# Hybrid decoder step: where one piece of query weights is staged, and when three groups of small instructions are issued

## The chip, the core and the metric

The kernel runs on one core of a Trainium2 chip. The metric is the device time of one execution in microseconds (us), the median of several runs. The core has a matrix engine (PE), a vector engine (DVE), a scalar engine (ACT), a general engine (POOL) and a queue engine (SP) that issues most of the DMA transfers. Each engine runs its own list of instructions in order and waits on semaphores for the others.

## The reference, cut to what matters

One layer of a hybrid decoder is computed for a prompt of 1,024 tokens and for 8 single new tokens ("samples") that have 2,048 cached tokens each. The model is 1,024 wide.

- The input is normalised (RMS norm) and multiplied with one matrix `w_in` of 1024 x 3864. Its columns give the gates of a short convolution, the queries (512 columns, eight heads of 64), keys and values of three branches, branch gates and an output gate.
- Queries and keys are normalised per head and rotated by position.
- Each query attends in three branches, which are mixed by sigmoid gates: over compressed blocks (32 tokens are turned into one key and value by the weights `cmp_w`), over the sixteen 64-token blocks that score best, and over a window of 512 tokens.
- The convolution group and the attention group are multiplied by their SiLU gates, put side by side, multiplied by `w_out` and added to the input.
- The samples do the same with cached rows, which are gathered by a page table, and the new cache rows are outputs too.

## The kernel before

Every product is made to nearly full fp32 precision from fast matmuls: each operand is split into a high and a low part (ACT copies the high part with `copy`, line 78, and DVE or POOL subtracts to get the low part with `sub`, line 82), and two or three matmuls are summed in PSUM. Transposes are matmuls against the identity.

**Order.** The Python text is written as several generators that are interleaved (`merge`). The written order is not the final one: when the program is built, a scheduler goes through it with modelled times and fixes each engine's list. An engine gets, among the instructions that the model calls ready, the one written earliest; buffers that share a name are handed out in the order written. So the place of a line sets its priority, and the model's idea of when data land decides the rest. On the chip the lists are then run strictly in order, whatever the real times are.

**Stage 1 (to about 232 us), `phase0` and `chan_stream`.** For each block of input columns the weights come in four pieces (`w_loader`, lines 162 to 191): `fetch` loads a piece of two k-tiles by a DMA of SP (line 171), `split` makes high and low tiles `wh` and `wl` of it. Raw pieces live in two buffers `wraw` and one `wx`; there are nine `wh` and nine `wl`, and a set needs eight. The columns are three key/value branches (`kv_tile`) and two halves of the queries (`q_tile`, the loop `for which in range(2)`), each over nine token tiles; the order of the tiles in the query loop is 0, 1, 2, 3, 8, 4, 5, 6, 7. Between them PE runs chunks of the channel products (`chan_mm`, lines 225 to 227). The weights of the second query half are fetched and split while the first half runs (lines 779 to 788): pieces 0 and 1 into `wraw`, piece 2 into `wx`, and piece 3 into a `wraw` again, after piece 0 is split. In the same loop `w_fetch` and `w_split` split one half of `w_out` and store it in DRAM: k-slices 0, 2, 4, 6 use the two buffers named `rows`, slices 1, 3, 5, 7 the two named `kd2`; a slice takes one buffer for the load and one for its high part.

In the first branch, pairs of token tiles are sent from SBUF to SBUF by four DMAs (`token_pairs`, line 432) and then transposed on PE (`cmp_transposes`, line 440). That second step is queued in a list `posts` with a count; every call of `posted(1)` takes one off, and what reaches zero is written out there (line 657). `small_things`, in the step of tile 7, queues `indices` with a count of 1: six small matmuls (lines 507 and 510). Both take PSUM banks of the name `tp`.

**Stage 2 (to about 660 us)** is the prompt's attention, with the convolution beside it.

**Stage 3 (about 670 to 790 us), `cmp_stream`**, builds the samples' compressed keys: in 16 steps, step n starts the gather of rows n + 2 into one of two buffers `raw`, `regroup(n + 1)` copies the next rows into one of two buffers `reg` (half by ACT, line 78, half by POOL, line 79, two copies each), and then four groups of four transposes (line 1149) and their products with `cmp_w` (line 1170) follow. Output products of the prompt (`out_tile`, lines 1582 to 1584) fill PE between them.

**Stage 4 (to the end), `sample_stream`**: for every 512 cached keys and each half h of the samples `keys` makes scores, `weigh` the softmax, and `values` transposes the weights into `ptz` (ACT line 78 for the high part, DVE line 82 for the low part) and multiplies them with the values (line 1466, 16 matmuls). After the last `values` an end part (lines 1498 to 1515) scales and sums the branches for h = 0 and for h = 1 on DVE and ACT and transposes the result on PE; the samples' output product (line 1617) follows. The prompt's last output tiles fill PE here too.

Of the kernel before, what the change touches and what calls it, by code (L numbers as in the profile page):

```python
# [10 lines left out]
F32 = mybir.dt.float32  # L11
# [50 lines left out]
def hymba_step_kernel(ctx, tc, io):  # L62
    nc = tc.nc
    WARM = 8

# [97 lines left out]
    def w_loader(wp, n, kp, raw_bufs, hk, hl_bufs, lo_eng=POOL):  # L163


        def load(col, width):
            hs, ls, raws = [], [], []

            def fetch(i, home=wp, name="wraw"):
                r = home.tile([128, kp, n], F32, name=name, bufs=raw_bufs if name == "wraw" else 1)  # L170
                SP.dma_start(r[:, :, :width], w_in[:, i * kp:(i + 1) * kp, col:col + width])
                raws.append(r)

            def split(i, eh=ACT, el=lo_eng):
                for j in range(0, kp, hk):
                    r = raws[i][:, j:j + hk, :width]
                    h = wp.tile([128, hk, n], F32R, name="wh", bufs=hl_bufs)
                    l = wp.tile([128, hk, n], F32R, name="wl", bufs=hl_bufs)
                    copy(eh, h[:, :, :width], r)
                    sub(el[j // hk % len(el)] if isinstance(el, tuple) else el, l[:, :, :width], r, f(h[:, :, :width]))  # L180
                    hs.append(h)
                    ls.append(l)

            def tiles(k):
                return hs[k // hk][:, k % hk, :width], ls[k // hk][:, k % hk, :width]

            return tiles, fetch, split
# [167 lines left out]
    ROWS, ENDS = 2, 14000  # L355
# [253 lines left out]
    def phase0():  # L609
# [36 lines left out]
        for t in range(NT):  # L646
# [9 lines left out]
            if rows is not None and t < 8:  # L656
                posts.append((lambda pr=token_pairs(rows, t - 1), t=t: cmp_transposes(pr, t - 1), 4 if t < 5 else 3 if t < 7 else 1))
# [110 lines left out]
        for which in range(2):  # L768
            w = nxt[0]
            nxt = wl0(COL_Q + 256, 256)  # L770
            for t in (0, 1, 2, 3, 8, 4, 5, 6, 7):
# [7 lines left out]
                if which == 0:  # L779
                    if t == 0:  # L780
                        for i in range(2):
                            nxt[1](i)
                        nxt[1](2, wk, "wx")
                    if t == 2:
                        nxt[2](0, ACT, EL)
                        nxt[1](3)
                    if t in (3, 4, 5):
                        nxt[2](t - 2, ACT, EL)
# [342 lines left out]
    def cmp_stream():  # L1131
# [64 lines left out]
        for n in range(16):  # L1196
            if n + 2 < 16:
                gather(n + 2)
            if n + 1 < 16:
                regroup(n + 1)  # L1200
# [6 lines left out]
            for j in range(2):  # L1207
                for rp in range(2):
# [92 lines left out]
    def sample_stream():  # L1301
# [135 lines left out]

        def values(c, h, Sb):
# [10 lines left out]
            sub(DVE, pz[:, :, 4:32:9, :], pv, f(pz[:, :, 0:28:9, :]))  # L1449
# [51 lines left out]
        for h in range(2):  # L1501
# [13 lines left out]
            PE.transpose(p[:, 32 * h:32 * h + 32], low[:, h], ident[:32, :32])  # L1515
        ms = sp_.tile([128, 4, 8], F32, name="ms")
# [247 lines left out]
```

## Time and profile before

| | |
|---|---|
| three runs, median (lowest to highest) | 920.47 us (914.07 to 924.98) |
| the profiled execution's own time | 922.36 us |
| its span | 920.6 us |
| mean granted TensorE clock | 0.978 of full speed |
| busy: PE, PE weight loads, DVE, ACT, POOL | 95%, 85%, 63%, 58%, 44% |

The profile is of one execution. Times on its lines count from the start of the span. The difference of 1.8 us between the execution's time and its span lies around the span. Busy times are shares of the whole span, which holds stages with different limits. A line of the timeline gives the start, the time that the group took, the engine, the source line, the operation with its output and inputs, how many instructions were merged, and in brackets how long the engine had been idle and what ended that wait.

### The profile page before, as it was taken

To read this page: it belongs to the slowest core of one execution; us is meant where nothing else is said; L and a number is where in the kernel's file an instruction comes from. 1 tells how busy PE (TensorE), PEld (TensorE's weight loads), DVE (VectorE), ACT (ScalarE), POOL (GpSimd) and SP (SyncE) were. 2 spreads that over 40 slices of the span, in tenths; PEclk is the share of its full clock that TensorE was granted. 3 is DMA by queue.
4 is the path that set the end of the run, shared out by engine and by line. 5 is a ranking of instruction groups with operands and counts; after the bars stand their busy time and mean duration, and the time that the engine had idled before them with its cause. 6 is when DMAs were issued, how large, how long until landed. Compare 5 with 4: busy or idle time off the path is not lost.

```text
span 920.6 us, 16583 instructions
## 1 busy us (share of the span) xinstructions
PE 874.4 (95%) x5769; PEld 784.8 (85%) x5769; DVE 576.8 (63%) x1482; ACT 532.7 (58%) x1350; POOL 400.5 (44%) x547
## 2 busy tenths in 40 slices
PE   8998999999899999999989999999989999999987
PEld 6898999989789889899979898999878788677765
DVE  5865627776555555765685677657745555765663
ACT  5552425433665655666565755666756776777761
POOL 4231303111454444544353543444654444677751
PEclk9998989989899999999999999999989999999999
DMA  7432402620011001220111000000977552667611
GB/s 261 127 96 71 120 10 77 223 80 21 16 30 36 24 24 46 70 69 13 59 58 24 24 12 13 24 1 7 274 263 270 198 193 94 239 214 245 221 67 48
DMA packets 67154, 91.14 MB, mean 99 GB/s; under 512 B 19191, under 2 KB 49343, under 8 KB 64894
## 3 DMA queue, kind: packets, MB, share of 16 engines
q1 hardware_dynamic: 58428, 52.16, 18.5%
q0 software_dynamic: 8064, 37.75, 12.3%
q8 instruction: 46, 0.75, 0.3%
q14 instruction: 38, 0.31, 0.1%
q10 hardware_dynamic: 578, 0.17, 0.1%
HBM read 77.92 MB, written 15.29 MB: 101 GB/s over the span
## 4 chain that ended last, share of the span: by engine, by line
PE 47%; ACT 7%; DVE 7%; issue 3%; POOL 3%; DMA 2%; SPq 0%; ACTq 0%; DVEq 0%; POOLq 0%
PE o L1024 7%; PE pt L1014 5%; PE s L940 5%; PE mm L227 5%; PE mm L225 5%; PE mm L226 5%; POOL P L989 2%; PE om L1170 2%; ACT P L930 1%; PE mm L1582 1%; PE mm L1583 1%; PE o L1466 1%; PE mm L1584 1%; PE pt L1149 1%; ACT ph L78 1%
## 5 line engine op out<-in xcount | busy, mean ns | idle before, releaser
L225 PE MATMUL mm<-hH,wh 128*128 128x384 f32 (+1 forms) x480 | 157.6, 328 | 2.3 <-ACT mixC L397 1.3
L227 PE MATMUL mm<-hH,wl 128*128 128x384 f32 (+1 forms) x480 | 154.9, 323 | 0.1
L226 PE MATMUL mm<-hL,wh 128*128 128x384 f32 (+1 forms) x480 | 154.6, 322 | 0.0
L82 POOL TENSOR_TENSOR wl<-wraw,wh 128x256 fp32r<-128x256 f32 (+1 forms) x105 | 78.1, 761 | 142.2 <-ACT wh L78 119.2
L930 ACT ACTIVATE P<-P,stat 128x640 f32<-128x640 f32 (+7 forms) x192 | 113.0, 590 | 38.1 <-DVE stat L928 37.5
L82 DVE TENSOR_TENSOR pl<-pt,ph 128x512 fp32r<-128x512 f32 (+1 forms) x164 | 102.8, 636 | 50.6 <-ACT ph L78 49.3
L78 ACT ACTIVATE ph<-pt 128x512 fp32r<-128x512 f32 (+1 forms) x164 | 88.4, 548 | 68.9 <-PE pt L1014 68.1
L989 POOL TENSOR_SCALAR P<-P,stat,gates 128x640 f32<-128x640 f32 (+7 forms) x128 | 100.3, 793 | 55.2 <-DVE stat L980 52.1
L1014 PE MATMUL pt<-ident,P 128*128 128x128 f32 x592 | 95.3, 279 | 6.1 <-POOL P L989 3.7
L940 PE MATMUL s<-k,q 128*128 128x320 f32 (+8 forms) x416 | 95.8, 333 | 1.9 <-DVE stat L928 1.9
L210 PE MATMUL mm<-wh,hH 128*128 128x256 f32 (+1 forms) x320 | 95.6, 299 | 1.3 <-ACT hH L78 0.7
L211 PE MATMUL mm<-wl,hH 128*128 128x256 f32 (+1 forms) x320 | 95.2, 297 | 1.7 <-DVE wl L82 0.9
L212 PE MATMUL mm<-wh,hL 128*128 128x256 f32 (+1 forms) x320 | 94.9, 296 | 1.2 <-DVE hL L82 1.2
L225 PEld LDWEIGHTS mm<-hH,wh 128*128 128x128 f32 x480 | 91.0, 190 | 3.3 <-ACT mixC L397 1.5
L227 PEld LDWEIGHTS mm<-hH,wl 128*128 128x128 f32 x480 | 91.3, 190 | 0.5 <-POOL wl L82 0.5
L226 PEld LDWEIGHTS mm<-hL,wh 128*128 128x128 f32 x480 | 91.3, 190 | 0.2
L928 DVE CUSTOM_DVE_ANT_0 P<-s,mask 128x32 f32<-128x32 f32 (+8 forms) x160 | 70.8, 473 | 26.2 <-PE s L940 22.3
L1014 PEld LDWEIGHTS pt<-ident,P 128*128 128x128 f32 x592 | 70.3, 140 | 19.3 <-POOL P L989 10.2
L1024 PE MATMUL o<-ph,v 128*128 128x256 f32 x264 | 74.5, 301 | 2.2 <-ACT ph L78 1.6
L1024 PE MATMUL o<-pl,v 128*128 128x256 f32 x264 | 73.4, 300 | 1.6 <-DVE pl L82 1.5
L940 PEld LDWEIGHTS s<-k,q 128*128 128x128 f32 x416 | 66.5, 190 | 6.1 <-PE pt L1014 1.6
L210 PEld LDWEIGHTS mm<-wh,hH 128*128 128x128 f32 x320 | 64.4, 201 | 2.4 <-ACT hH L78 1.4
(385 smaller groups left out, 2064.9 us busy)
## 6 DMA issues: line engine op xcount, KB each, us to landing
wraw<-in_w_in_dram SPq DMA_DIRECT2D x54, 256.0 KB
wo<-wo_d POOLq DMA_DIRECT2D x8, 512.0 KB, 5.7
out_s_win_dram<-in_state_win_kv_dram SPq DMA_DIRECT2D x8, 511.0 KB
xr<-in_x_prompt_dram SPq DMA_DIRECT2D x14, 256.0 KB
out_y_prompt_dram<-xr SPq DMA_DIRECT2D x14, 256.0 KB
sd<-in_state_win_kv_dram SPq DMA_DIRECT2D x5, 512.0 KB
mixA<-in_x_prompt_dram SPq DMA_DIRECT2D x4, 512.0 KB
xt<-in_x_prompt_dram SPq DMA_DIRECT2D x4, 512.0 KB
```

The lines of the kernel that those rows point to most:

```text
L78: return ACT.activation(out, in_, AF.Copy)
L82: return eng.tensor_tensor(out, a, b, OP.subtract)
L210: PE.matmul(o[:, :n], hH[t // 3][:, k, s], wh, start=k == 0, stop=False)
L211: PE.matmul(o[:, :n], hH[t // 3][:, k, s], wl, start=False, stop=False)
L225: PE.matmul(o[:, :n], wh, hH[c][:, k], start=k == 0, stop=False)
L226: PE.matmul(o[:, :n], wh, hL[c][:, k], start=False, stop=False)
L227: PE.matmul(o[:, :n], wl, hH[c][:, k], start=False, stop=k == 7)
L930: return lambda: ACT.activation(P, P, AF.Exp, bias=stt[:, 0, c:c + 1], scale=-1.0, accum_out=stt[:, 1, c:c + 1])
L940: PE.matmul(s[:, a:b], q[:, i], k, start=first, stop=not first)
L989: POOL.tensor_scalar(P[:, i, :n], P[:, i, :n], stt[:, 2, c + i:c + i + 1], gates[:, qi, gt:gt + 1], op0=OP.mult, op1=OP.mult)
L1014: PE.transpose(p[:, y * 256 + i * 128:y * 256 + i * 128 + 128], src[:, i], ident)
L1024: PE.matmul(o[0][:, :256], v, X[:, y * 256:y * 256 + 256], start=br == 1 and x == 0 and y == 0 and X is h[0], stop=last and y + 1 == len(p ...
```

## The change

Four edits.

1. **Fourth piece of the second queries' weights.** `fetch` learns to load a piece into a buffer of the name `rows` (a room of 512 columns, which holds two k-tiles of 256). Piece 3 of the second query half is no longer fetched into `wraw` right behind the split of piece 0, in the step of tile 2, but into `rows` in the step of tile 5. Its split is written in the step of tile 7 instead of tile 5; the splits of pieces 0 to 2 stay. The constant `ROWS` moves to the top.
2. **Last pair's transposes.** The count with which the transposes of the pair of tiles 6 and 7 are queued is 2 instead of 1, so they are written one `posted` later: behind the chunk of channel products that follows tile 8, and behind `indices`.
3. **Regrouping.** `regroup(n + 1)` is written between the two halves of step n (before the transposes of j = 1) instead of at its start.
4. **The end of the first rows.** The end part becomes a function `ends(h)`. The DVE instructions of `ends(0)` get an ordering edge: they stand on DVE's list behind the subtraction that makes the last `ptz` (an edge of order only; nothing waits for its completion). `ends(1)` has none.

```diff
--- before.py
+++ after.py
@@ -62,6 +62,7 @@
 def hymba_step_kernel(ctx, tc, io):
     nc = tc.nc
     WARM = 8
+    ROWS = 2
 
     keep = tc.keep_in_program_order
     PE, ACT, DVE, POOL, SP = nc.tensor, nc.scalar, nc.vector, nc.gpsimd, nc.sync
@@ -167,7 +168,10 @@
             hs, ls, raws = [], [], []
 
             def fetch(i, home=wp, name="wraw"):
-                r = home.tile([128, kp, n], F32, name=name, bufs=raw_bufs if name == "wraw" else 1)
+                if name == "rows":
+                    r = home.tile([128, 512], F32, name=name, bufs=ROWS).rearrange("p (k n) -> p k n", k=kp)
+                else:
+                    r = home.tile([128, kp, n], F32, name=name, bufs=raw_bufs if name == "wraw" else 1)
                 SP.dma_start(r[:, :, :width], w_in[:, i * kp:(i + 1) * kp, col:col + width])
                 raws.append(r)
 
@@ -352,7 +356,7 @@
     wp = ExitStack()
     wk = wp.enter_context(pool("w0", "right"))
     rope0 = mCf[:, 0:1152].rearrange("p (i t d) -> p i t d", i=2, t=NT)
-    ROWS, ENDS = 2, 14000
+    ENDS = 14000
 
     wk.tile([128, 512], F32, name="rows", bufs=ROWS)
     wk.tile([128, 2, 280], F32, name="wx")
@@ -654,7 +658,7 @@
             posted(1)
             rows = kv_tile_rows(t, 0, tab0)
             if rows is not None and t < 8:
-                posts.append((lambda pr=token_pairs(rows, t - 1), t=t: cmp_transposes(pr, t - 1), 4 if t < 5 else 3 if t < 7 else 1))
+                posts.append((lambda pr=token_pairs(rows, t - 1), t=t: cmp_transposes(pr, t - 1), 4 if t < 5 else 3 if t < 7 else 2))
             if t == 5:
                 tab1 = rope_tables(io["k_gain"][0, 1], 1, 1.0)
                 small_loads()
@@ -781,11 +785,12 @@
                         for i in range(2):
                             nxt[1](i)
                         nxt[1](2, wk, "wx")
+                    if t == 5:
+                        nxt[1](3, wk, "rows")
                     if t == 2:
                         nxt[2](0, ACT, EL)
-                        nxt[1](3)
-                    if t in (3, 4, 5):
-                        nxt[2](t - 2, ACT, EL)
+                    if t in (3, 4, 7):
+                        nxt[2]({3: 1, 4: 2, 7: 3}[t], ACT, EL)
                 yield ENDS if t == 7 else 1300
         posted(9)
 
@@ -1196,8 +1201,6 @@
         for n in range(16):
             if n + 2 < 16:
                 gather(n + 2)
-            if n + 1 < 16:
-                regroup(n + 1)
             if n in (4, 7, 10):
                 next(start, None)
             if n == 11:
@@ -1205,6 +1208,8 @@
                 for _ in range(NSW):
                     load(*next(ahead))
             for j in range(2):
+                if j and n + 1 < 16:
+                    regroup(n + 1)
                 for rp in range(2):
                     pend.append((n, j, rp) + transposes(n, j, rp))
                     if len(pend) > CD:
@@ -1435,6 +1440,8 @@
                 ACT.activation(su, su, AF.Identity, bias=cs, scale=fac[0:32, h, br:br + 1])
             return Sb
 
+        last = [None]
+
         def values(c, h, Sb):
 
             br = 1 if c == 4 else 0
@@ -1446,7 +1453,7 @@
             pz = ptz[h]
             pv = p[:, :128].rearrange("p (t b r) -> p t b r", t=4, b=4)
             copy(ACT, pz[:, :, 0:28:9, :], pv)
-            sub(DVE, pz[:, :, 4:32:9, :], pv, f(pz[:, :, 0:28:9, :]))
+            last[0] = sub(DVE, pz[:, :, 4:32:9, :], pv, f(pz[:, :, 0:28:9, :]))
             products(0)
             if ext:
                 p = bank("pt")
@@ -1498,7 +1505,7 @@
         fin = ep.tile([64, 2, 128], F32, name="srows1")
         low = ep.tile([32, 2, 128], F32, name="srows2")
         p = bank("pt")
-        for h in range(2):
+        def ends(h):
             for br in range(2):
                 z = stats[:, h, br]
                 DVE.tensor_scalar(z[:, 5:6], z[:, 4:5], 1e-30, None, op0=OP.max)
@@ -1513,6 +1520,10 @@
             copy(ACT, low[:, h], fin[32:64, h])
             DVE.tensor_tensor(low[:, h], low[:, h], fin[0:32, h], OP.add)
             PE.transpose(p[:, 32 * h:32 * h + 32], low[:, h], ident[:32, :32])
+
+        with tc.issue_after(last[0].ins):
+            ends(0)
+        ends(1)
         ms = sp_.tile([128, 4, 8], F32, name="ms")
         pv = p[:, :64].rearrange("p (b g h e) -> p g e h b", b=8, g=2, h=2)
         for g in range(2):
```

## Rows read from the trace of the kernel before

**Rows 1.** Part 1 of the page: busy time, share and instructions of each engine.

```profile
PE 874.4 (95%) x5769; PEld 784.8 (85%) x5769; DVE 576.8 (63%) x1482; ACT 532.7 (58%) x1350; POOL 400.5 (44%) x547
```

**Rows 2.** Waits of PE: line, awaited, total us, times, longest us.

```profile
PE o L1466 <- DVE ptz L82: 2.5, 1, 2.5
...
PE tp L440 <- DVE rb L275: 2.3, 1, 2.3
...
PE om L1170 <- DVE xl L82: 1.6, 5, 0.3
```

**Rows 3.** Timeline of PE, second query half.

```profile
192.12 0.39 PE L210 MATMUL mm<-wh,hH 128*128 128x256 f32 x1 [0.51 <-ACT wh L78]
...
193.31 0.39 PE L211 MATMUL mm<-wl,hH 128*128 128x256 f32 x1 [0.80 <-POOL wl L82]
...
194.86 0.58 PE L211 MATMUL mm<-wl,hH 128*128 128x256 f32 x1 [0.94 <-DVE wl L82]
...
201.13 0.28 PE L210 MATMUL mm<-wh,hH 128*128 128x256 f32 x1
...
206.46 0.34 PE L225 MATMUL mm<-hH,wh 128*128 128x384 f32 x1
```

**Rows 4.** Busy time by window: PE, PEld, DVE, ACT, POOL, granted clock, DMA, GB/s.

```profile
196.00:198.00 2.00, 2.00 (x11) 2.00 (x11) 1.37 (x5) 0.81 (x3) 0.00 (x0) 0.50 0.00 0
```

**Rows 5.** Timeline of SP, ACT and DVE, around the second queries' weights.

```profile
171.43 0.46 SPq L757 DMA_DIRECT2D rows<-in_w_out_dram  x1
...
188.91 0.38 SPq L171 DMA_DIRECT2D wraw<-in_w_in_dram  x1
...
187.20 0.63 ACT L266 ACTIVATE rb<-q 128x512 f32<-128x512 f32 x1 [2.59 <-DVE q_s L277]
...
191.66 0.72 ACT L78 ACTIVATE wh<-wraw 128x256 fp32r<-128x256 f32 x2 [1.10 <-DMA wraw<-in_w_in_dram]
...
183.26 0.69 DVE L82 TENSOR_TENSOR rows<-rows 128x512 fp32r<-128x512 f32 x1
```

**Rows 6.** Timeline of SP and PE, around the last pair's transposes.

```profile
67.18 2.60 SPq L432 DMA_DIRECT2D pr<-rows  x4
...
71.35 1.09 PE L440 MATMUL tp<-ident,pr 128*128 128x128 f32 x4 [2.33 <-DVE rb L275]
72.37 0.59 PE L507 MATMUL tp<-ptT,spread 16*128 16x8 f32 x2
72.82 0.99 PE L510 MATMUL tp<-ptT,spread 16*128 16x4 f32 x4
...
78.15 0.28 PE L210 MATMUL mm<-wh,hH 128*128 128x256 f32 x1
```

**Rows 7.** Stage 3: its window, and one regrouping on ACT and POOL.

```profile
690.00:790.00 100.00, 95.94 (x640) 82.53 (x639) 54.62 (x105) 67.95 (x136) 48.28 (x61) 1.00 0.54 186
...
707.69 1.14 ACT L78 ACTIVATE reg<-raw 128x512 f32<-128x512 f32 x2
...
708.53 1.16 POOL L79 COPY reg<-raw 128x512 f32<-128x512 f32 x2
```

**Rows 8.** Timeline of DVE, ACT, POOL and PE, last values and end part.

```profile
893.65 1.43 DVE L1510 SCALAR_TENSOR_TENSOR acc<-acc,fac 64x256 f32<-64x256 f32 x1
...
897.32 0.27 DVE L82 TENSOR_TENSOR ptz<-pt,ptz 128x128 fp32r<-128x128 f32 x1
...
902.35 0.48 DVE L1510 SCALAR_TENSOR_TENSOR acc<-acc,fac 64x256 f32<-64x256 f32 x1 [0.73 <-ACT fac L1507]
...
894.22 0.28 ACT L78 ACTIVATE ptz<-pt 128x128 fp32r<-128x128 f32 x1
...
894.75 1.44 POOL L82 TENSOR_TENSOR ml<-mixA,mh 128x512 fp32r<-128x512 f32 x1
...
886.46 1.10 PE L1466 MATMUL o<-vhl,ptz 128*64 128x256 f32 x8
...
897.64 3.47 PE L1466 MATMUL o<-vhl,ptz 128*64 128x256 f32 x16 [2.54 <-DVE ptz L82]
```

## The prediction

> **What bounds the kernel now.** Read first the busy times on the page: PE works 95% of the span, no other engine over 63% [rows 1]. So only what leaves PE waiting, or slows its clock, can pay, and the next view to read is the list of PE's own waits. Three of its entries are touched by this change: the transposes of the last pair (line 440), the value products (line 1466) and the products of stage 3 (line 1170) [rows 2]. The waits for the second queries' weights are split over three smaller entries, so they are found in the timeline of PE instead, where three waits of 0.51, 0.80 and 0.94 us stand close together [rows 3]. What the list does not tell is what follows such waits: in the window behind them PE is busy all the time, yet the granted clock is 0.50, so the level is 1.2 instead of 2.4 GHz [rows 4]. A wait is therefore to be priced with the stretch of half clock behind it.
>
> **Edit 1, the fourth piece.** From 192.12 to 201.13 us PE starts 33 matmuls of the same shape (six left of the first tile, 24 of the second, three of the third): 9.01 us. From 201.13 to 206.46 it starts 45: 5.33 us, or 0.118 us each [rows 3]. At that pitch the 33 take 3.9 us. Lost are 5.1 us and the 0.51 us of the first wait: 5.6 us. The cause is in the lists of the other engines: SP issues the fourth piece only at 188.91, when piece 0 has left its buffer, and ACT waits 1.10 us for it to land before the last two splits at 191.66 [rows 5]. With `rows` as home the fetch waits instead for the stores of `w_out` slice 2. That buffer comes free at 171.43, where slice 4 now takes it [rows 5], some 17 us before the split is due. Then the last two splits can stand right behind the others, and PE, which needs 18 matmuls or 2.1 us for the first three pieces, meets finished tiles.
>
> What is queued behind: while piece 3 sits in the room, the high parts of slices 4 and 6 have no buffer, so two `w_split`s move from before 187 us to behind the last split, with about 0.6 us on ACT, 0.69 us on DVE and two stores on SP each. One of them, the DVE subtraction at 183.26, now stands in the chain that ACT waits for at 187.20 [rows 5]; taking it out lets the splits begin up to 0.7 us earlier. What stands behind the moved ones are copies of query sums out of PSUM and the rotations, which PE does not wait for until three banks are full (two tiles each). Their stores are read only in stage 2. So I take the whole 5.6 us: **-5.6**. Bounds: -5.6, and 0 if the moved splits put the same wait elsewhere.
>
> **Edit 2, the transposes.** PE waits 2.33 us at 71.35 for the pair's DMAs, issued from 67.18, and full pace returns at 78.15 [rows 6]. In these 6.8 us it runs the four transposes (1.0 us), the six matmuls of `indices` (72.37 to 73.74, 1.4 us) and 20 weight products. At full clock they would take about 1.2 + 20 x 0.118 = 3.6 us, so the place costs 2.33 + 3.2 = 5.5 us. But I do not expect the wait to go. The chunk of channel products behind which the transposes are now written already runs before them, because in the builder's model the DMAs had not landed; what comes next, the first tile of the second branch, is written behind them before and after. So they should keep about their place, ahead of their data. What does move is `indices`: written first now, its six matmuls run before the wait and fill a part of it. That frees 1.4 us at half clock behind it, worth 0.7 us, less a matmul or so that then falls behind: **-0.6**. Bounds: -5.5 if the wait and the half clock go, and +0.5 if the three small DVE copies that follow `indices` get in front of the chain that issues the DMAs.
>
> **Edit 3, regrouping.** In the middle of stage 3 PE is busy 95.94 of 100 us at full clock [rows 7], so at most 4 us are there to win. The entry that this edit can touch is the 1.6 us of five waits for DVE's `xl` [rows 2]: two ACT copies of 1.14 us together [rows 7] stand ahead of the evictions that `xl` needs. Since an idle ACT takes the copies early anyway, I take a quarter: **-0.4**. Bounds: -1.6, and +1.2 for one pair of copies late once. The gather that refills the other `raw` buffer starts half a step later, but it has two steps (some 7 us each) to land, as before.
>
> **Edit 4, the end of the first rows.** ACT has the last `ptz` high part ready at 894.50; DVE subtracts at 897.32, because it first runs the end of the first rows, whose line 1510 alone takes 1.43 us [rows 8]. PE waits 2.54 us, and then its 16 products take 3.47 us, where eight took 1.10 us before [rows 8]: at that pace 2.2. So 2.54 + 1.27 = 3.8 us lie here, and all that follows to the end (the second rows' end, the samples' output product, the last output tile) hangs behind these products. Behind the `ptz` subtraction the first rows' chain must still run, about five DVE steps and ACT's four scalings, and its transposes stand in PE's list. Line 1510 takes 0.48 us at 902.35, and 1.43 us beside POOL's subtraction of 1.44 us [rows 8]; I let this 0.95 us come back as a wait of PE: **-2.9**. Bounds: -3.8, and 0.
>
> The Trainium skill bears on that 0.95 us: SBUF — State Buffer, section "Who interferes with whom", says that a DVE instruction with two inputs in SBUF and a GpSimd instruction that reads SBUF hold each other out entirely, whichever starts first going first. The trace agrees, with 1.43 against 0.48 us for one form. By that rule an order edge moves the blocking with the chain and does not remove it; if it held all five DVE steps for one POOL subtraction more, this edit would give -2.4 instead of -2.9.
>
> **The sum.** -5.6 - 0.6 - 0.4 - 2.9 = -9.5 us. The profiled execution took 922.36 us, so it would be 912.9. It lay 1.9 us above the median of the three runs; taken from the median of 920.47 the forecast is **911.0 us**. PE is the bound between the places, so I carry the gains to the end without loss: ahead of the attention ACT and DVE wait for PE, and later stages follow PE.
>
> **Rivals.**
>
> *The pair's wait goes after all* (-5.5 instead of -0.6). For it: the transposes do get a later place in the text. Against it: the chunk already runs ahead of them. 911.0 - 4.9 = 906.1 us. Chance 0.15.
>
> *The moved splits of `w_out` take the place of the wait.* ACT runs in order; a copy of slice 4 or 6 that waits for its load holds the copies of query sums behind it, as ACT stood 2.59 us at 187.20 [rows 5]. One such wait of PE, 2.59 us, and no more half clock saved than lost: edit 1 gives about -2.6. 914.0 us. Against it: three PSUM banks of slack. Chance 0.17.
>
> *The first rows' transposes stop PE.* PE's list has them where the model thinks the chain is done; if it is late by as much as now, the 2.54 us return [rows 8], and edit 4 gives -1. Then 912.9. Chance 0.14; it differs little from the forecast.
>
> *Regrouping comes too late* (the one on the other side). The copies for the next step now have half a step. If POOL's pair, 1.16 us [rows 7], ends after PE's last transposes of the step, PE waits every step: 15 x 1.16 = 17.4 us more, and 911.0 + 0.4 + 17.4 = 928.8 us, slower than before. It decides when the pair starts later than 1.16 us ahead of the step's end, for instance behind one of POOL's long subtractions. Against it: POOL is busy 48 of 100 us there [rows 7]. Chance 0.06, in part beyond 1%.
>
> **How the numbers follow.** The forecast itself has a chance of 0.48. The line of 1%, about what a measurement of this kernel can tell from no change, lies at 911.3 us, next to the forecast: so half of its chance counts as faster and half as the same, a bit less than half for the first of it and the third rival going the other way. Faster: 0.15 + 0.48 x 0.55 + 0.03 = 0.45. Slower by over 1%: 0.04, from the last rival. Same: the rest, 0.51. The range reaches from 904.5 (the first rival with the better bound of edit 3) to 917.5, where edit 1 falls to nothing and the rest holds (911.0 + 5.6 = 916.6) with a little for the spread of the runs; regrouping too late is left out.
>
> **What would show it.** Edit 1: the load of piece 3 issued near 171 us, no wait on `wl` of piece 3, and a granted clock of 1.00 from 190 to 232. Edit 2: lines 507 and 510 ahead of line 440, and a wait on line 440 still there at half clock behind it; if there is none, the first rival holds. Edit 3: fewer waits on `xl`, and none of line 1149 on `reg`. Edit 4: `ptz` at once behind ACT's copy, 16 value products in about 2.2 us, lines 1510 to 1512 behind it. The prediction is wrong if the time saved at 190 us is given back before the attention starts, or if stage 3 shows waits on `reg`.

## The result and the profile after

The changed kernel takes **910.46 us** (median of ten runs, 907.66 to 911.83); the kernel before 922.21 us (median of ten runs, the three of the table above among them). The ratio is 0.9878, with a 95% interval of 0.9852 to 0.9904: clear of no change, and faster by 1.2%. The forecast was 911.0 us, 9.5 us below the 920.47 us of three runs; the ratio gives a gain of 11.3 us (8.9 to 13.6). So the time was met more closely than the gain, since the starting point moved up by 1.7 us. The sum was right within its interval; two of its four terms were not, and they erred in opposite directions. In the ratios here and below two runs far above all others of their kernel are left out, one of the kernel before (2,843 us) and one of edit 4 alone (1,487 us).

The profiled execution took 910.97 us (span 908.4, mean granted clock 0.992; before 922.36, 920.6 and 0.978). The source lines have moved by 1 (`copy` is 79, `sub` 83) to 11.

Part 1 of the page of the changed kernel, against [rows 1]:

```profile
PE 863.8 (95%) x5769; PEld 773.6 (85%) x5769; DVE 578.0 (64%) x1482; ACT 534.0 (59%) x1350; POOL 402.5 (44%) x547
```

PE's busy time fell by 10.6 us with the same number of instructions: between these two executions, most of what was won are matmuls at the higher level of the clock, not idle time. How much of that is the edits' and how much the draw of an execution is taken up below.

Waits of PE in the changed kernel (columns as in [rows 2]):

```profile
PE om L1175 <- ACT xh L79: 3.9, 2, 2.7
...
PE om L1175 <- DVE xl L83: 1.6, 4, 0.5
PE tp L444 <- DVE rs L202: 1.5, 1, 1.5
...
PE mm L229 <- ACT wh L79: 1.1, 1, 1.1
PE ptx L1522 <- DVE srows L1521: 1.0, 2, 0.8
```

The wait for `ptz` is gone, the wait of the pair's transposes (now line 444) is 1.5 instead of 2.3 us, the waits for `xl` are what they were, and a wait of 1.1 us for `wh` on line 229 is new.

To see where time was won, match the n-th product of a line in one trace with the n-th in the other and follow the difference of their starts along the span. It is 3.9 us at 79 us of the kernel before (the pair), 5.4 at 125, 9.7 at 202 (second queries), 7.0 at 250, 6.4 at 675, 8.9 at 686, 7.4 at 705, 9.0 at 775 (stage 3), 8.6 at 890 and 12.2 at the end. The steps at 79 (edit 2), 202 and 250 (edit 1), 775 (edit 3) and the end (edit 4) belong to edits. Those at 125 and 686 us stand where no edit is, and the 1.5 us lost by 705 us, with a new wait of 1.2 us for `xh`, are not in the trace of edit 3 alone (below).

**The pair.** PE around the transposes, to set beside [rows 6]:

```profile
63.89 0.38 PE L511 MATMUL tp<-ptT,spread 16*128 16x8 f32 x2
64.14 0.58 PE L514 MATMUL tp<-ptT,spread 16*128 16x4 f32 x4
...
71.31 0.63 PE L444 MATMUL tp<-ident,pr 128*128 128x128 f32 x4 [1.49 <-DVE rs L202]
71.69 0.36 PE L214 MATMUL mm<-wh,hH 128*128 128x256 f32 x1
```

The six products of `indices` run ahead of the chunk of channel products, six weight products (seven before) stand between that chunk and the transposes, and the transposes take 0.63 instead of 1.09 us: full clock. Windows of the changed kernel (busy PE, PEld, DVE, ACT, POOL, granted clock, DMA share, GB/s), behind the pair, at the second queries' weights, and in the middle of stage 3, against [rows 4, 7]:

```profile
72.00:78.00 6.00, 6.00 (x53) 6.00 (x52) 4.03 (x6) 2.13 (x5) 3.33 (x2) 1.00 0.24 60
190.00:196.00 6.00, 6.00 (x53) 6.00 (x52) 4.70 (x12) 2.44 (x5) 0.00 (x0) 1.00 0.42 143
196.00:202.00 6.00, 6.00 (x41) 5.92 (x41) 4.42 (x11) 1.57 (x4) 0.00 (x0) 1.00 0.11 44
682.60:782.60 100.00, 95.65 (x641) 82.30 (x640) 57.08 (x108) 69.59 (x140) 48.37 (x60) 1.00 0.56 194
```

**The fourth piece.** SP and ACT in the changed kernel, against [rows 5]:

```profile
166.65 0.46 SPq L175 DMA_DIRECT2D rows<-in_w_in_dram  x1
167.44 0.34 SPq L761 DMA_DIRECT2D rows<-in_w_out_dram  x1
...
184.70 0.71 ACT L79 ACTIVATE wh<-rows 128x256 fp32r<-128x256 f32 x2
```

Piece 3 is asked for 22 us sooner, its splits stand right behind the others, and PE's three waits of 0.51, 0.80 and 0.94 us [rows 3] have become two of 0.43 and 0.17. But further on, DVE, ACT and PE:

```profile
189.06 0.69 DVE L83 TENSOR_TENSOR rows<-rows 128x512 fp32r<-128x512 f32 x1
...
195.00 0.68 DVE L83 TENSOR_TENSOR rows<-rows 128x512 fp32r<-128x512 f32 x1
...
217.30 0.63 ACT L270 ACTIVATE rb<-q 128x512 f32<-128x512 f32 x1 [2.35 <-DVE q L281]
217.83 0.71 ACT L79 ACTIVATE wh<-wraw 128x256 fp32r<-128x256 f32 x2
...
218.29 0.45 PE L229 MATMUL mm<-hH,wh 128*128 128x384 f32 x1 [1.06 <-ACT wh L79]
```

The two moved subtractions stand among the rotations of the query sums. PE is now 9.7 us ahead of its old time, the rotations only 5 to 6; ACT waits 2.35 us for the rotation before it can square the next sums, and the splits for the next channel products are behind that in its order. From here to 245 us of the kernel before 2.6 us are given back.

**The end.** DVE, PE and POOL, against [rows 8]:

```profile
885.60 0.27 DVE L83 TENSOR_TENSOR ptz<-pt,ptz 128x128 fp32r<-128x128 f32 x1
...
886.30 2.03 PE L1473 MATMUL o<-vhl,ptz 128*64 128x256 f32 x16
...
890.65 0.21 PE L1522 MATMUL ptx<-ident,srows 32*128 32x32 f32 x1 [0.23 <-DVE srows L1521]
...
893.02 0.24 PE L1522 MATMUL ptx<-ident,srows 32*128 32x32 f32 x1 [0.78 <-DVE srows L1521]
...
887.78 0.48 DVE L1517 SCALAR_TENSOR_TENSOR acc<-acc,fac 64x256 f32<-64x256 f32 x1
...
889.03 0.27 DVE L1519 TENSOR_TENSOR srows<-acc 64x128 f32<-64x128 f32 x1
...
890.88 1.43 DVE L1519 TENSOR_TENSOR srows<-acc 64x128 f32<-64x128 f32 x1
...
890.87 1.29 POOL L83 TENSOR_TENSOR ml<-mixC,mh 128x512 fp32r<-128x512 f32 x1 [3.46 <-ACT mh L79]
```

PE does not wait for `ptz`, and 16 products take 2.03 instead of 3.47 us. The transposes of the two rows now cost 0.23 + 0.78 us of waiting (0.66 before): 0.35 us came back. The second row's wait is DVE's line 1519, 1.43 us beside POOL's 1.29 and 0.27 alone. That is the rule of the Trainium skill (SBUF — State Buffer, section "Who interferes with whom") at work, but not as the prediction feared. The first rows' chain has lost its blocking: its line 1517 (1510 before) takes 0.48 us, where it took 1.43. The second rows' chain was blocked before as well, on another line:

```profile
903.99 1.14 DVE L1514 TENSOR_TENSOR srows<-srows,srows 32x128 f32<-32x128 f32 x1 [0.40 <-ACT srows L78]
...
903.70 1.29 POOL L82 TENSOR_TENSOR ml<-mixC,mh 128x512 fp32r<-128x512 f32 x1 [7.50 <-ACT mh L78]
```

So the edge did not carry the blocking along with the chain; of the 0.35 us, 0.12 are the difference between these two waits of the second row.

### The profile page after: what moved, and what is told of

The parts are those of the page before. It is cut to its first block, busy times and chain, and to the rows that moved or that the text cites. A ratio compares the mean times of both kernels' runs of the same rounds, so it can differ in the third digit from the quotient of the medians.

```text
span 908.4 us, 16577 instructions
## 1 busy us (share of the span) xinstructions
PE 863.8 (95%) x5769; PEld 773.6 (85%) x5769; DVE 578.0 (64%) x1482; ACT 534.0 (59%) x1350; POOL 402.5 (44%) x547
## 4 chain that ended last, share of the span: by engine, by line
PE 48%; ACT 7%; DVE 7%; issue 3%; POOL 3%; DMA 2%; SPq 1%; ACTq 0%; DVEq 0%; POOLq 0%
PE o L1029 7%; PE pt L1019 5%; PE s L945 5%; PE mm L231 5%; PE mm L230 5%; PE mm L229 5%; POOL P L994 2%; PE om L1175 2%; DMA wor<-in_w_out_dram 1%; ACT P L935 1%; PE mm L1593 1%; PE pt L1154 1%; PE mm L1594 1%; PE mm L1595 1%; ACT ph L79 1%
## 5 line engine op out<-in xcount | busy, mean ns | idle before, releaser
L216 PE MATMUL mm<-wh,hL 128*128 128x256 f32 (+1 forms) x320 | 92.2, 288 | 1.3 <-DVE hL L83 1.3
L214 PE MATMUL mm<-wh,hH 128*128 128x256 f32 (+1 forms) x320 | 93.0, 291 | 0.1
L215 PE MATMUL mm<-wl,hH 128*128 128x256 f32 (+1 forms) x320 | 92.3, 288 | 0.6 <-DVE wl L83 0.6
L1019 PEld LDWEIGHTS pt<-ident,P 128*128 128x128 f32 x592 | 70.3, 140 | 19.6 <-POOL P L994 10.2
L216 PEld LDWEIGHTS mm<-wh,hL 128*128 128x128 f32 x320 | 61.6, 192 | 1.7 <-DVE hL L83 1.7
```

Of the source, the lines that this page charges most:

```text
L214: PE.matmul(o[:, :n], hH[t // 3][:, k, s], wh, start=k == 0, stop=False)
L216: PE.matmul(o[:, :n], hL[t // 3][:, k, s], wh, start=False, stop=k == 7)
L1019: PE.transpose(p[:, y * 256 + i * 128:y * 256 + i * 128 + 128], src[:, i], ident)
```

## The experiments

Ratios are to the kernel before, run on the same chip, with 95% intervals. "Lost to half clock" is, averaged over a kernel's runs, its span times (1 - mean granted clock), which each run lists; the kernel before loses 15.7 us so (77 runs), the changed kernel 9.4 (ten runs). It is an upper bound of what the half clock costs, since it also counts half-clock time in which PE waits: over the 77 runs, a run that loses 1 us more by this measure has a span 0.68 us longer.

| kernel | median us | ratio | lost to half clock |
|---|---|---|---|
| edit 1 alone | 916.63 | 0.9962 [0.9945, 0.9980] | 12.4 |
| edit 2 alone | 917.13 | 0.9959 [0.9941, 0.9978] | 12.7 |
| edit 3 alone | 919.71 | 0.9996 [0.9973, 1.0019] | 15.7 |
| edit 4 alone | 918.00 | 0.9972 [0.9955, 0.9988] | 13.6 |
| all, subtractions on POOL | 914.42 | 0.9926 [0.9900, 0.9951] | 12.0 |
| all, pair's count 4 | 910.25 | 0.9890 [0.9864, 0.9916] | 10.4 |
| all, `indices` late | 913.94 | 0.9935 [0.9912, 0.9958] | 12.7 |
| all, compression in two places | 912.66 | 0.9903 [0.9876, 0.9929] | 9.4 |
| all, the first place later | 910.01 | 0.9866 [0.9829, 0.9902] | 9.4 |
| all, second `rb` | 907.06 | 0.9842 [0.9804, 0.9881] | 8.6 |
| all, count 4, two places, second `rb` | 903.00 | 0.9801 [0.9761, 0.9841] | 6.2 |
| second `rb` alone | 920.99 | 0.9985 [0.9961, 1.0008] | 15.1 |

Stretches of half clock in the one trace of each kernel, in us (windows of 0.5 us); a dash is none:

```
place:                   pair  compression  2nd queries  attention  stage 3  last values
before                    6.8     10.2          6.8         6.8       6.8       3.4
edit 1 alone              6.8      6.8           -          6.8       6.8       3.4
edit 2 alone               -       6.8           -          6.8       3.4       3.4
edit 3 alone              6.8     10.2          3.4         6.8        -        3.4
edit 4 alone              6.8     10.2          3.4         6.8        -         -
all                        -       6.8           -          6.8        -         -
all, POOL                  -       6.8          3.4         6.8       3.4        -
all, count 4               -      10.2           -          6.8        -         -
all, indices late         6.8     10.2           -          6.8       3.4        -
all, two places            -       6.8           -          6.8       3.4        -
all, first place later     -       3.4           -          6.8       6.8        -
all, second rb             -      10.2           -           -         -         -
all, three more            -       3.4           -           -        3.4        -
second rb alone           3.4     10.2           -          3.4        -         -
```

The compression's stretch stands at 96.5 us with two places, and three of the traces (POOL, count 4, two places) have one more of 3.4 us near 462 us.

**Edit 1 alone.**

```diff
+                    if t == 5:
+                        nxt[1](3, wk, "rows")
...
-                        nxt[1](3)
-                    if t in (3, 4, 5):
-                        nxt[2](t - 2, ACT, EL)
+                    if t in (3, 4, 7):
+                        nxt[2]({3: 1, 4: 2, 7: 3}[t], ACT, EL)
...
```

> Edit 1 alone. Theory (from matching the products of TensorE one by one in the two traces): the stop at 192 us goes and 4.3 us are won by 201 us, but 2.6 us are given back near 225 us, where TensorE waits for the weights of the next channel products because the rotations of the query sums on VectorE now end the wait; 1.6 us remain, ratio to the kernel before 0.998. Rival A (the prediction): the whole 5.6 us stay, ratio 0.994. Rival B: the give-back belongs to the other edits, and 4.3 us stay, ratio 0.995. The wait of 2.33 us on line 440 and the half clock behind it, and the wait of 2.54 us on line 1466, should stand as before.

Measured: 3.5 us (1.8 to 5.1). The window behind the splits is at full clock, and the wait for the next weights is there without the other edits:

```profile
196.00:202.00 6.00, 6.00 (x51) 6.00 (x50) 4.70 (x12) 2.05 (x4) 0.00 (x0) 1.00 0.36 131
```

```profile
222.54 0.45 PE L229 MATMUL mm<-hH,wh 128*128 128x384 f32 x1 [1.04 <-ACT wh L79]
```

So the give-back belongs to edit 1, and rival B's reason falls. The theory has the mechanism, but its 1.6 us lie below the interval, and rival B's 4.3 us inside it: the runs won more than the trace. This execution was one of the slowest of its twelve (919.37 us) and lost 15.6 us to half clock where the twelve lose 12.4 on average. The whole 5.6 us lie outside the interval.

**Edit 2 alone.**

```diff
... the count at the end of the line:
-4 if t < 5 else 3 if t < 7 else 1
+4 if t < 5 else 3 if t < 7 else 2
```

> Edit 2 alone. Theory: the products of the indices stand in the wait, which falls from 2.33 to about 1.5 us, and no stretch of half clock follows it; 3.9 us won by 79 us, ratio 0.996. Rival (the prediction): the half clock stays, 0.6 us, ratio 0.999. Open: whether the further 1.5 us that the changed kernel won between 112 and 123 us, in a stretch of half clock that ended sooner, comes with this edit (then 5.4 us by 125 us, 0.994) or with none.

Measured: 3.8 us (2.0 to 5.4), no half clock behind the pair. The further 1.5 us by 125 us are in this trace, but also in that of edit 1 alone, whose code there is that of before; so they are not shown to be this edit's. The trace also shows what a single trace is worth at the second queries: edit 1 is absent, PE stops three times (0.30, 0.73, 0.94 us), and no half clock follows:

```profile
190.00:196.00 6.00, 5.95 (x50) 5.96 (x51) 4.67 (x11) 1.91 (x4) 0.00 (x0) 1.00 0.01 3
196.00:202.00 6.00, 6.00 (x44) 6.00 (x44) 4.20 (x11) 1.91 (x4) 0.00 (x0) 1.00 0.00 0
```

**Edit 3 alone.**

```diff
-            if n + 1 < 16:
-                regroup(n + 1)
...
+                if j and n + 1 < 16:
+                    regroup(n + 1)
```

> Edit 3 alone. Theory: 1.6 us won in the middle of stage 3 (727 to 770 us of the kernel before), ratio 0.998, by fewer waits for line 1170's low parts; and the 2.5 us that the changed kernel won at 680 us, where a stretch of half clock behind the first wait of stage 3 is missing, are not this edit's, since the code is the same there. Rival: they are (ratio 0.996). Prediction: 0.4 us, ratio 1.000.

Measured: 0.4 us, with an interval on both sides of none. In the middle of its stage 3 PE is busy 97.06 of 100 us (95.94 before [rows 7]; but 95.65 in the changed kernel, where the new wait of 1.2 us for `xh` falls):

```profile
686.00:786.00 100.00, 97.06 (x650) 83.82 (x649) 57.29 (x109) 69.33 (x141) 50.33 (x61) 1.00 0.56 200
```

The start of stage 3 was at full clock here, and with edit 4 alone as well, whose code there is that of before: that step of the ladder is not this edit's.

**Edit 4 alone.**

```diff
-            sub(DVE, pz[:, :, 4:32:9, :], pv, f(pz[:, :, 0:28:9, :]))
+            last[0] = sub(DVE, pz[:, :, 4:32:9, :], pv, f(pz[:, :, 0:28:9, :]))
...
-        for h in range(2):
+        def ends(h):
...
+        with tc.issue_after(last[0].ins):
+            ends(0)
+        ends(1)
```

> Edit 4 alone. Theory: the wait of 2.54 us for the last ptz goes, 16 value products take 2.0 instead of 3.5 us, 0.4 us come back as two short waits for the transposed rows: 3.5 us, ratio 0.996. Rival (the prediction): 0.95 us come back, 2.9 us, ratio 0.997. Until 890 us nothing should differ from the kernel before.

Measured: 2.6 us (1.1 to 4.1). PE:

```profile
893.38 2.03 PE L1468 MATMUL o<-vhl,ptz 128*64 128x256 f32 x16
...
900.06 0.24 PE L1517 MATMUL ptx<-ident,srows 32*128 32x32 f32 x1 [0.78 <-DVE srows L1516]
```

The four alone make 3.5 + 3.8 + 0.4 + 2.6 = 10.3 us, and the product of their ratios is 0.9889; all together gave 0.9878. Within their intervals they add up.

**All four, `indices` behind the pair again.**

```diff
-        posts.append((indices, 1))
+        posts.append((indices, 3))
```

> All four edits, but the products of the indices fall due two steps later, behind the pair's transposes again. Theory: it is the length of TensorE's stop that decides on the half clock behind it; without the 6 products in the gap the stop is 2.3 us again and a stretch of half clock of about 6.8 us stands behind it: 3 to 4 us more than the changed kernel, ratio to the kernel before 0.992. Rival: the stretch went for another reason (the place of the transposes, a better start of the tile), the stop is 2.3 us and full clock follows: 0.8 us more, 0.989.

Measured: 0.9935, where the changed kernel has 0.9878. PE's stop and the window behind it:

```profile
71.50 1.09 PE L444 MATMUL tp<-ident,pr 128*128 128x128 f32 x4 [2.34 <-DVE rb L279]
```

```profile
70.60:71.07 0.47, 0.00 (x0) 0.00 (x0) 0.44 (x3) 0.00 (x0) 0.00 (x0) 1.00 0.57 138
71.10:71.50 0.40, 0.00 (x1) 0.04 (x1) 0.36 (x3) 0.00 (x0) 0.33 (x1) 0.50 0.88 302
72.00:78.00 6.00, 6.00 (x28) 5.65 (x27) 2.41 (x6) 1.12 (x2) 2.04 (x2) 0.51 0.23 61
```

The same six products, moved back, bring back both the stop of 2.3 us and the 6.8 us of half clock, and 3.9 us are lost by 80 us. The theory holds. One rival is near: the six small products, which now run behind the stop again, could be what brings the clock down. But here the clock fell before they ran: it is 0.50 from 71.1 us, while PE still stands, and they begin at 72.5. In the traces of the kernel before and of edit 3 alone it also fell within the stop; in the other three traces with the long stop it fell 0.1 to 1.5 us behind its end.

**All four, the moved subtractions on POOL.**

```diff
-            sub(DVE, l, f(l), f(h))
+            sub(POOL if k in (4, 6) else DVE, l, f(l), f(h))
```

> All four edits, and the subtractions of the two moved slices of w_out go from VectorE to GpSimd. Theory: in the changed kernel these two, 0.69 us each, and the rotations behind them make the chain of the query sums end at 217.2 us, and the splits that follow on ScalarE hold TensorE for 1.06 us at 218.3 us; without them the chain ends 1.4 us sooner and this wait falls below 0.3 us: 1 to 1.4 us less than the changed kernel, ratio to the kernel before 0.986. Rival: GpSimd's subtractions stop VectorE's two-input steps beside them for as long, and nothing is won (0.988). The wait for wh near 218 us decides it in the trace.

Measured: 0.9926, slower than with DVE; the wait for `wh` is 1.46 us. Nothing is won, for the rival's reason, and more is lost than its 0.988 says:

```profile
190.75 1.84 DVE L279 TENSOR_TENSOR rb<-qn,mixC 128x256 f32<-128x256 f32 x2
...
191.02 1.29 POOL L83 TENSOR_TENSOR rows<-rows 128x512 fp32r<-128x512 f32 x1 [2.28 <-ACT rows L79]
```

The pair of DVE instructions that takes 0.75 us alone takes 1.84 beside POOL's subtraction: again the rule of the Trainium skill (SBUF — State Buffer, "Who interferes with whom"). But not all of the loss is theirs. Ahead of them ACT waits for the load of a slice of `w_out`, 2.95 us here and 1.98 in the changed kernel, and the samples' rotation stands behind it in ACT's order:

```profile
178.45 0.63 ACT L79 ACTIVATE kd<-kd 128x512 fp32r<-128x512 f32 x1 [2.95 <-DMA kd<-in_w_out_dram]
```

In this trace the weights' splits begin later, PE stops 0.76 and 0.45 us at 186 us, and 3.4 us of half clock follow. That is the mechanism of the prediction's second rival, at a slice that the change did not move. Why the load came later, and whether it did in the other runs, is open.

**All four, second `rb`.** (The second buffer lies in a piece of `mixC` that is free by then.)

```diff
-            r = wk.tile([128, 512], F32, name=name)[:n, :m * nh * 64]
+            if name == "rb" and rbx:
+                rbx.reverse()
+            r = rbx[0] if name == "rb" and rbx and rbx[0] is not None else wk.tile([128, 512], F32, name=name)
+            r = r[:n, :m * nh * 64]
...
+        rbx.extend([mCf[:, 3456:3968], None])
```

> All four edits, and the rotations of the query sums take turns on two buffers of squares (rb) instead of one, so that ScalarE squares the next sums while VectorE still rotates. Theory: after the edits the queries' rotations, one after the other at 5.4 to 5.9 us each, end at 217.2 us and set the wait of 1.06 us at 218.3 us; with two buffers a rotation takes about 0.8 us less, the chain catches up with TensorE, and this wait goes: about 1 us less than the changed kernel, ratio to the kernel before 0.987. Rival: the wait is for the weights' load or for ScalarE's other copies, and stays (0.988).

Measured: 907.06 us, 0.9842. This is more than the 1 us expected, but the interval (0.9804 to 0.9881) holds the theory's ratio and the rival's. The trace decides: ACT squares and splits in time, PE has no wait for `wh` there, and by 227 us 2.6 us more are won than in the changed kernel, 2.4 of them behind 215 us: all that was given back by then. By the same matching of products, in every trace with edit 1 and one buffer 2.3 us (3.2 with the subtractions on POOL) are given back between 217 and 237 us of the kernel before; in the six others, those with two buffers or without edit 1, it is 0.1 us at most. The start of the attention is at full clock too, in this trace:

```profile
214.71 0.63 ACT L274 ACTIVATE rb<-q 128x512 f32<-128x512 f32 x1
215.25 0.71 ACT L79 ACTIVATE wh<-wraw 128x256 fp32r<-128x256 f32 x2
```

```profile
224.00:236.00 12.00, 10.14 (x61) 8.42 (x59) 7.82 (x33) 8.02 (x31) 3.70 (x9) 1.00 0.01 1
```

**Second `rb` alone**, on the kernel before; the same edit as above.

> The kernel before with the second buffer of squares (rb) alone, none of the four edits. Theory: without edit 1 TensorE is late at 201 us, the rotations keep up with it and the splits near 225 us come in time, so the buffer wins nothing of the 2.6 us that it won on the changed kernel by 225 us: ratio to the kernel before 0.999 or 1.000, and the only thing it may change is the stretch of half clock of 6.8 us at 235 us. Rival: the buffer is worth its 3.4 us by itself, whatever edit 1 does: 0.996.

Measured: 0.9985, not to be told from no change. By the traces the buffer pays only behind edit 1, which made the rotations the bound. This trace also has the kernel before's stop for the last `ptz`, and no half clock behind it, where the kernel before took 3.47 us [rows 8]:

```profile
893.18 2.08 PE L1471 MATMUL o<-vhl,ptz 128*64 128x256 f32 x16 [2.55 <-DVE ptz L82]
```

**All four, pair's count 4.**

```diff
... the end of the same count:
-3 if t < 7 else 2
+3 if t < 7 else 4
```

> All four edits, and the last pair's transposes fall due two steps later (4 instead of 2), behind 18 more products. Theory: the wait of 1.49 us on line 444 goes, nothing else is late: 1.5 us less than the changed kernel, ratio to the kernel before 0.986. Rival: the copies of the pair's transposes and of the indices now come later, and a wait of the same size stands at the channel products of the first tile of the second branch or at the compression near 104 us (0.988).

Measured: 0.9890, the same as the changed kernel. The wait is gone and nothing took its place, yet in the trace 1.9 us won by 79 us are gone at 120, where the clock was half for 10.2 us instead of 6.8:

```profile
71.56 0.60 PE L444 MATMUL tp<-ident,pr 128*128 128x128 f32 x4
```

```profile
106.00:116.00 10.00, 10.00 (x47) 10.00 (x47) 5.39 (x23) 1.75 (x7) 0.05 (x1) 0.50 0.29 79
```

The runs lose 10.4 us to half clock on average against 9.4, so this may be a draw of those runs; it stays open.

**All four, the compression's 64 narrow products in two places.**

```diff
+            if t == 6:
+                cmp_products(0)
...
-        for j in range(2):
-            o = gps[:, j * 512:j * 512 + 512]
-            for rho in range(16):
...
+        cmp_products(1)
```

> All four edits, and the 64 products of 66 columns of the compression, which run in one piece from 104 to 115 us, stand in two places, 32 after the seventh tile of the second branch and 32 where all were. In every trace so far the clock falls to half some 4.5 us after the first of them and stays there for 6.8 or 10.2 us (0.50 in the window 110 to 114 us of the changed kernel). Theory: it is the run of narrow products that brings the clock down; two runs of 3.6 us each do not, and 3.4 us or more are won: ratio to the kernel before 0.984. Rival: each run brings it down by itself, nothing is won or 3 us lost (0.988 to 0.991).

Measured: 0.9903. The first run waits 0.9 us for its weights and has 6.8 us of half clock behind it, the second has none:

```profile
92.00:96.00 4.00, 3.17 (x30) 3.05 (x28) 2.50 (x10) 1.11 (x2) 0.26 (x1) 1.00 0.39 105
97.00:103.00 6.00, 6.00 (x21) 6.00 (x21) 0.55 (x2) 0.00 (x0) 0.00 (x0) 0.50 0.33 92
112.00:116.00 4.00, 4.00 (x38) 4.00 (x37) 3.83 (x9) 2.73 (x9) 3.50 (x6) 1.00 0.63 176
```

**The same, the first place one tile later** (`t == 7`).

> As the version with the compression's products in two places, but the first 32 stand one tile later, where the compression's weights have long been split, so that no wait of 0.9 us falls among them. Theory: there it was this wait with the narrow products behind it that brought the clock down for 6.8 us at 96.5 us, and the second 32 alone did not; now neither does, and the 6.8 or 10.2 us of half clock of all earlier traces are gone: 3.4 us less than the changed kernel, ratio to the kernel before 0.984. Rival: narrow products bring the clock down in 3.6 us too, and one stretch of 6.8 us stands behind the first 32: 0.988.

Measured: 0.9866. Now the first run is clean and the second is followed by 3.4 us:

```profile
104.00:111.00 7.00, 7.00 (x63) 6.97 (x62) 4.94 (x11) 4.25 (x12) 3.14 (x4) 1.00 0.52 148
112.00:115.00 3.00, 3.00 (x15) 3.00 (x15) 2.83 (x9) 1.26 (x5) 2.29 (x4) 0.51 0.56 154
```

Shorter, not gone: neither theory as stated, and no gain that the runs can tell.

**All four with count 4, the first place later and second `rb`.** The three edits above, together.

> All four edits, with the last pair's transposes due at 4 instead of 2, two buffers of squares, and the compression's products in two places, the first one tile later. Theory: the waits of 1.49 us at 71 us and 1.06 us at 218 us and the half clock at 110 us go together: 1.5 + 1.1 + 3.4 us less than the changed kernel, ratio to the kernel before 0.981. Rival: what is won ahead is taken back by a longer stretch of half clock elsewhere, as in the version with the later transposes alone: 0.986 to 0.988.

Measured: **903.00 us** (901.07 to 906.54), 0.9801 [0.9761, 0.9841]. Every run lies below the lowest of the changed kernel (907.66), though that was timed on another occasion. The theory's size is met (0.981), its parts only in part: the waits at 71 and 218 us are gone, but 3.4 us of half clock remain at 110 us, and what makes up for them, the half clock at the attention, it did not count. The attention starts at full clock again:

```profile
220.00:236.00 16.00, 13.02 (x79) 10.59 (x78) 9.08 (x36) 10.44 (x38) 7.63 (x17) 1.00 0.00 1
```

## Why the prediction was right in the sum and wrong in two terms

| edit | forecast | alone, by the runs | in the trace of all four |
|---|---|---|---|
| 1 | -5.6 | -3.5 (-1.8 to -5.1) | -4.3, then +2.6 |
| 2 | -0.6 | -3.8 (-2.0 to -5.4) | -3.9 |
| 3 | -0.4 | -0.4 (-2.5 to +1.7) | -1.6 at 727 to 775 us |
| 4 | -2.9 | -2.6 (-1.1 to -4.1) | -3.5 |
| sum | -9.5 | -10.3 | -12.2 with the steps that no edit owns |

**Edit 2: the step that failed** is the half clock behind the pair's wait. The prediction saw that `indices` would move ahead and fill a part of the wait, and that the transposes would keep their place; both are so. It took it that the stretch of half clock would stay, because a wait stayed. But a stop of 1.49 us is not one of 2.33 us: with the longer stop the stretch was there in six traces of six (3.4 or 6.8 us), with the shorter or none it was in none of eight. The experiment that moved the six products back shows that they decide it. The missing term is the whole stretch: 6.8 us at half clock are 3.4 us, besides the 0.84 us of stop. The first rival (-5.5) came nearer, but lies just outside the interval, and its way, the wait gone altogether, is not what happened.

**Edit 1: two steps failed.** First, "the rotations, which PE does not wait for until three banks are full". At 218 us PE does not wait for the rotations themselves; ACT does, and the splits of the next weights stand behind in ACT's order. With PE 9.7 us ahead the rotations, which follow one another through one buffer `rb` at about 5.5 us each with two subtractions of 0.69 us among them, were late for the first time. The two subtractions are the smaller part: from each of the two rotations at which they stand to the next it is 6.2 and 5.9 us, and at the same two in the trace of edit 2 alone, without them, 6.1 and 5.5. The second `rb` took the give-back away, and won nothing that can be told without edit 1. The prediction had named this as its sign of being wrong, time saved at 190 us and given back before the attention: 2.3 of the 4.3 us were, by 237 us of the kernel before, where the attention has just begun.

The second rival named the moved splits and ACT's order and gave -2.6; its mechanism, a copy of a slice that waits for its load, is there too (1.42 us at 193.54 us, 1.98 us for another slice at 176.06), but in the changed kernel PE did not stop for it.

Second, the price of the stop: up to 3.4 of the 5.6 us were the half clock behind it in one execution. In five traces without edit 1 that stretch was 6.8, 3.4, 3.4 us and twice nothing, at the same place: 2.7 us of stretch, 1.4 us of time, on average. Taken together the two explain too much: 5.6 less 2.6 and 2.0 is 1.0 us, and the runs of edit 1 alone show 3.5 (1.8 to 5.1). Both steps are in the traces; where the runs win the other 2.5 us is open.

**Edit 3** was sized as measured, but the interval is wider than the effect. The entry it was costed by, the waits for `xl`, is 1.6 us before and after, but not with the same waits: three of 0.34, 0.26 (both for `xl`) and 0.58 us (for `kco`) between 729 and 734 us, which stand in the traces of edits 1, 2 and 4 alone too, are gone here and with edit 3 alone, and others for `xl` ahead of them (0.47 and 0.42 us at 674 and 686 us) fill the sum up again. The rival that regrouping comes too late did not happen: PE waits for no `reg`.

**Edit 4** went as forecast: wait gone, products at 2.03 us (2.2 was taken). 0.35 us came back where 0.95 was allowed. The reason given for the 0.95 does not hold: in the kernel before line 1510 ran mostly beside POOL's subtraction ahead of the one shown (893.12 to 894.80 us), and behind the edge the first rows' chain is not blocked at all. The rival that the first rows' transposes stop PE is there with 0.23 us. The 1.27 us for slow products were not certain to be there: of the five traces that have this stop one, that of the second `rb` alone, has full clock behind it.

So the sum came out because the two errors, +2.1 and -3.2 us, nearly cancel. That is luck: nothing in the prediction ties the one to the other.

## What to carry to other kernels

Price a stop of TensorE by its length and by what follows it, and ask for each edit whether the stop gets short enough to lose the slow stretch behind it; filling a gap with a microsecond of unrelated matmuls was worth nearly four here. Take the length of that stretch from several executions, or from the granted clock that every run lists, not from one trace. And when TensorE gets ahead at one place, look one stage on for the chain that kept pace with it only because it was late: here one scratch buffer more took the measured gain from 1.2% to 1.6% (the intervals overlap).

## What the runs showed of the hardware that was not expected

Stretches of half clock inside the spans lasted about 3.4, 6.8 or 10.2 us and no other length, at the same code one or another or none from trace to trace (the table above). The length of a stop does not decide alone: a stop of 2.3 us at the pair was followed by half clock in six traces of six, one of 2.5 us at the last values in four of five. And a stretch can come without any stop: in all eleven traces in which 64 products of 66 columns, at 0.11 us each, ran in one piece, the clock fell to 0.50 while they ran, with PE busy all the time:

```profile
110.00:112.00 2.00, 2.00 (x11) 2.00 (x11) 1.56 (x9) 0.20 (x1) 0.00 (x0) 0.50 0.97 296
```

(the changed kernel). Cutting them into two pieces did not end this: a stretch stood at one of the pieces in each of three traces, 6.8 us where a stop of 0.9 us fell among them and 3.4 us in the other two. The mean span fell from 919.0 (77 runs of the kernel before) to 907.8 us, and the loss to half clock by 6.3 of these 11.2 us. That is an upper bound; at 0.68 us of span for each, as over the 77 runs, it is an estimate of 4.3 us. So some two fifths to a little over half of what four edits on waits brought is the clock behind the waits.
